# The block exchanges of a one-core decoder layer: issued by GpSimd's queue instead of SyncE's

## The chip, the cores and the metric

The kernel runs on one core of a Trainium2 chip. The metric is the device time of one execution in microseconds, median of several. The engines are named as the profile names them: PE is TensorE, with PEld its weight loads; DVE is VectorE, ACT is ScalarE, POOL is GpSimd, and SP is SyncE, which computes nothing and issues DMAs. A "q" behind a name (SPq, POOLq) means the engine's instruction queue.

## What is computed

One layer of a decoder over 256 tokens of width 2048, in float32: a half SwiGLU, a mixer with attention and spatial gating side by side, another half SwiGLU, and a last norm.

```python
def swiglu(x, w_gate, w_up, w_down):
    return (jax.nn.silu(x @ w_gate) * (x @ w_up)) @ w_down

x = x + 0.5 * swiglu(rmsnorm(x, ffn1_norm), ffn1_w_gate, ffn1_w_up, ffn1_w_down)   # D_FF = 5632
h = rmsnorm(x, mix_norm)
proj = h @ w_in                          # q, k, v, u, v_sg, gate_att, gate_sg
# attention: 3 groups of 4 heads, dilations 1, 4, 16, merged by their denominators
y_att = o_att @ w_att_out
# spatial gating in chunks of 128 positions: u * (W_s LN(v) + b)
y_sg = (u * spatial) @ w_sg_out
x = x + (sigmoid(g_att) * y_att + sigmoid(g_sg) * y_sg) @ w_out
x = x + 0.5 * swiglu(rmsnorm(x, ffn2_norm), ffn2_w_gate, ffn2_w_up, ffn2_w_down)
out = rmsnorm(x, final_norm)
```

## The kernel before

**Products.** Each weight matrix is read once, in units of 512 rows by 512 columns (1 MB, tile `raw`, three buffers, `load_unit`, line 121). A unit is worked off in two half-units of 256 rows. There are 776 half-units, and the program is one loop over them (line 838). To keep float32's precision on the faster float32r path, each half-unit is split: ScalarE rounds the weights to `wh` (line 139), VectorE subtracts to get the rest `wl` (line 140). The activations have been split in the same way (`xhi`, `xlo` and so on). A half-unit is 12 matmuls of 512 columns on TensorE (line 149), per 128 rows and token tile in the order wh·hi, wl·hi, wh·lo. So the first matmul needs `wh` and the second needs `wl`. `wh` and `wl` have four buffers: ScalarE may split three half-units ahead of the one that TensorE works on, and waits for TensorE to release a buffer.

**Exchanges.** A product leaves its result with tokens on the partitions, and the next product needs it with features on the partitions. That turn is done without TensorE, in `turn` (line 168). VectorE transposes 32x32 blocks into a tile `bt...` (`put`, line 191 or 197); one DMA writes the tile to a DRAM tile `bm...` (line 175, 512 KB, 128 partitions of 4 KB); four DMAs read it back with the blocks in turned order (line 181, 128 KB each, into 32 partitions, rows of 1 KB). Then ScalarE and VectorE split what came back (line 163 and 164, or a copy of that kind), which is called the evacuation here. The tiles' names tell the user: `h` is a block of hidden units (22 exchanges, back into `sg`), `x` the residual before a norm (8, into `xt`; there the evacuation begins with ScalarE's line 264), `u`, `q`, `k`, `p` and `m` belong to the mixer (3, 3, 3, 4 and 4), `w` is the spatial weight (2, of 384 KB). That makes 49 exchanges, so 49 writes and 196 reads.

**Order.** All of this order is written out by hand. After the products of half-unit i the loop runs what was registered with `at(i, ...)`: the transposes and the write of an exchange at i, its four reads at i + 3, its evacuation at i + 8, or at i + 6 for x and p. Then `advance` adds the loads and the splits of later half-units. Every engine takes its instructions in that order; a DMA that must wait for data (the reads for the write, the write for the transposes) holds the queue that issues it. SP's queue holds the weight loads, the exchanges and a few constants. POOL's has 18 busy instructions: constants, the powers of the norms (lines 226, 393, 732), the attention mask's rows (lines 341 to 348) and a triangular select of the spatial weights (line 366).

Of the kernel before, what the change touches and what calls it, by code (L numbers as in the profile page):

```python
# [41 lines left out]
def layer(ctx: ExitStack, tc: tile.TileContext, a, out):  # L42
    nc = tc.nc
    PE, ACT, DVE, POOL, SP = nc.tensor, nc.scalar, nc.vector, nc.gpsimd, nc.sync
# [9 lines left out]
    def tp_bank(name):  # L54
        return ps.tile([P, NC], F32, tag="tp", bufs=4, name=name)
# [60 lines left out]
    def at(i, fn):  # L116
        callbacks.setdefault(i, []).append(fn)
# [50 lines left out]
    def turn(i, name, q, put, dst, ev, lag=8):  # L168
        got = {}

        def blocks():
            d = sb.tile([P, 4, q, 32], F32, tag="gate", bufs=2, name=f"bt{name}")
            put(d)
            m = got["m"] = dram.tile([P, 4, q * 32], F32, tag="turn", name=f"bm{name}")
            SP.dma_start(m, d.rearrange("p j m b -> p j (m b)"))

        def back():
            got["e"] = e = dst()
            m = got["m"].rearrange("(i a) j r -> j a i r", a=32)
            for j in range(4):  # L180
                SP.dma_start(e[32 * j:32 * j + 32].rearrange("p (i r) -> p i r", i=4), m[j])

        at(i, blocks)
        at(i + 3, back)
        at(i + lag, lambda: ev(got["e"].rearrange("p (i m b) -> p m i b", i=4, b=32)))
# [589 lines left out]
    b = tp_bank("gc0")  # L775
# [130 lines left out]
```

## Time and profile before

| | us |
|---|---|
| time, median of three runs | 2047.57 (2047.5 to 2048.29) |
| the profiled execution, its own time | 2047.7 |
| its span, first to last instruction | 2046.0 |
| TensorE busy | 2035.8 |
| VectorE busy | 1182.3 |
| ScalarE busy | 974.5 |
| GpSimd busy | 12.5 |

A profile row of an engine gives the start and the length of an instruction in us, the engine, the line of the code, the operation, and the tiles as written<-read; "x4" are four instructions in one row, and a bracket behind it is the idle time before it and who ended it. A DMA's row stands on the queue that issues it and lasts as long as the issue, not as the transfer.

### The profile page before, as it was taken

How to read it: one execution, taken by the hardware profiler on the slowest of the kernel's cores; microseconds unless marked ns; L12 is line 12 of the kernel's file. 1: busy time of each engine (PE TensorE's matmuls, PEld its weight loads, DVE VectorE, ACT ScalarE, POOL GpSimd, SP SyncE). 2: the span in 40 equal slices, each digit the busy share in tenths (PEclk: the TensorE clock that was granted, in tenths of full speed). 3: DMA queues.
4: the chain of work that ended last, by engine and by line, in shares of the span. 5: the costliest groups of instructions: out<-in, count | busy, mean ns of one | idle time of the engine just before them, and what ended most of it. 6: DMA issues, size and time to landing. Idle time of an engine off the chain costs nothing.

```text
span 2046.0 us, 23823 instructions
## 1 busy us (share of the span) xinstructions
PE 2035.8 (100%) x9494; PEld 1781.4 (87%) x9494; DVE 1182.3 (58%) x1193; ACT 974.5 (48%) x1071; POOL 12.5 (1%) x18
## 2 busy tenths in 40 slices
PE   9999999999999999999999999999999999999998
PEld 7888888888888888888888888888888888888887
DVE  5555555455555657665665555565555555555554
ACT  6444444444445555455554444564444444444443
POOL 0000000000000000000000000000000000000000
PEclk9999999999999999999999999999999999999999
DMA  7776876566766855787766666776676656667664
GB/s 271 234 236 226 270 245 216 201 223 225 243 231 217 269 201 202 241 276 261 261 222 220 224 225 206 246 256 231 221 242 224 225 206 205 224 222 240 231 214 144
DMA packets 246775, 469.35 MB, mean 229 GB/s; under 512 B 11084, under 2 KB 38536, under 8 KB 246536
## 3 DMA queue, kind: packets, MB, share of 16 engines
q1 hardware_dynamic: 246344, 467.30, 68.8%
q8 instruction: 74, 1.21, 0.2%
q10 hardware_dynamic: 320, 0.53, 0.1%
q14 instruction: 37, 0.30, 0.0%
HBM read 439.22 MB, written 28.57 MB: 229 GB/s over the span
## 4 chain that ended last, share of the span: by engine, by line
PE 99%; issue 0%; ACT 0%; DVE 0%; POOLq 0%; POOL 0%
PE mm L149 98%; PE sp L458 0%; PE warm L772 0%; PE pv L624 0%; PE sc L587 0%; PE xt L235 0%; PE sc L585 0%; PE pv L620 0%; ACT x L740 0%; ACT xhi L239 0%; PE pv L621 0%; DVE x L725 0%; POOLq L901 0%; POOL rf L732 0%; ACT wh L139 0%
## 5 line engine op out<-in xcount | busy, mean ns | idle before, releaser
L140 DVE TENSOR_TENSOR wl<-raw,wh 128x1024 fp32r<-128x1024 f32 (+1 forms) x780 | 947.6, 1218 | 822.7 <-ACT wh L139 817.6
L139 ACT ACTIVATE wh<-raw 128x1024 fp32r<-128x1024 f32 (+1 forms) x780 | 817.9, 1052 | 1007.6 <-PE mm L149 976.7
L149 PE MATMUL mm<-wh,xhi 128*128 128x512 f32 x2144 | 814.0, 380 | 0.5 <-ACT wh L139 0.4
L149 PE MATMUL mm<-wh,xlo 128*128 128x512 f32 x2144 | 812.5, 379 | 0.0
L149 PE MATMUL mm<-wl,xhi 128*128 128x512 f32 x2144 | 811.8, 379 | 0.0
L149 PEld LDWEIGHTS mm<-wh,xhi 128*128 128x128 f32 x2144 | 405.2, 189 | 58.6 <-ACT wh L139 0.9
L149 PEld LDWEIGHTS mm<-wl,xhi 128*128 128x128 f32 x2144 | 405.4, 189 | 57.3
L149 PEld LDWEIGHTS mm<-wh,xlo 128*128 128x128 f32 x2144 | 405.2, 189 | 57.4
L149 PE MATMUL mm<-wl,hhi 128*128 128x512 f32 x704 | 266.8, 379 | 0.0
L149 PE MATMUL mm<-wh,hhi 128*128 128x512 f32 x704 | 266.8, 379 | 0.0
L149 PE MATMUL mm<-wh,hlo 128*128 128x512 f32 x704 | 266.8, 379 | 0.0
L149 PEld LDWEIGHTS mm<-wl,hhi 128*128 128x128 f32 x704 | 133.1, 189 | 18.9
L149 PEld LDWEIGHTS mm<-wh,hlo 128*128 128x128 f32 x704 | 133.1, 189 | 18.9
L149 PEld LDWEIGHTS mm<-wh,hhi 128*128 128x128 f32 x704 | 133.1, 189 | 18.9
L149 PE MATMUL mm<-wh,uT 128*128 128x512 f32 x192 | 58.0, 379 | 0.0
L149 PE MATMUL mm<-wh,mhi 128*128 128x512 f32 x128 | 48.5, 379 | 0.0
L149 PE MATMUL mm<-wl,mhi 128*128 128x512 f32 x128 | 48.5, 379 | 0.0
L149 PE MATMUL mm<-wh,mlo 128*128 128x512 f32 x128 | 48.5, 379 | 0.0
L149 PEld LDWEIGHTS mm<-wh,uT 128*128 128x128 f32 x192 | 36.3, 189 | 5.1
L149 PE MATMUL mm<-wl,uT 128*128 128x512 f32 x96 | 36.4, 379 | 0.0
L304 DVE SCALAR_TENSOR_TENSOR sg<-mm,rstd,sg 128x512 f32<-128x512 f32 x44 | 30.9, 743 | 0.0
L219 ACT ACTIVATE junk<-x 128x512 bf16<-128x512 f32 x30 | 18.9, 629 | 25.0 <-DVE x L247 18.6
(152 smaller groups left out, 600.6 us busy)
## 6 DMA issues: line engine op xcount, KB each, us to landing
raw<-in_w_in_dram SPq DMA_DIRECT2D x92, 1024.0 KB, 5.0
raw<-in_ffn_w_up_dram SPq DMA_DIRECT2D x88, 1024.0 KB, 5.1
raw<-in_ffn_w_down_dram SPq DMA_DIRECT2D x88, 1024.0 KB, 5.1
raw<-in_ffn_w_gate_dram SPq DMA_DIRECT2D x84, 1024.0 KB, 5.0
raw<-in_w_out_dram SPq DMA_DIRECT2D x16, 1024.0 KB, 5.1
raw<-in_w_sg_out_dram SPq DMA_DIRECT2D x12, 1024.0 KB, 5.7
bmh<-bth SPq DMA_DIRECT2D x22, 512.0 KB, 2.7
sg<-bmh SPq DMA_DIRECT2D x88, 128.0 KB, 4.9
```

Of the source, the lines that this page charges most:

```text
L139: ACT.activation(wh[:, k], r[:, k], AF.Copy)
L140: DVE.tensor_tensor(wl[:, k], r[:, k], wh[:, k].bitcast(F32), op=OP.subtract)
L149: PE.matmul(g["ps"][t], act[:, k, t * P:(t + 1) * P], in_turn(w[:, jj]), start=k == 0 and kind == "hh", stop=k == g["nk"] - 1 and kind == ...
L219: ACT.activation(junk, x[:, t, c * NC:(c + 1) * NC], AF.Square, accum_out=ss[n][:, t, c:c + 1])
L304: DVE.scalar_tensor_tensor(two(sg[:, t]), banks[t], rstd[:, t:t + 1], two(sg[:, t]), op0=OP.mult, op1=OP.mult)
```

## The change

In `turn`, the write and the four reads of every exchange are started from GpSimd's queue. Nothing else is altered: the callbacks, their places, the tiles, the shapes of the transfers and the other engines' orders are the same.

```diff
         def blocks():
             d = sb.tile([P, 4, q, 32], F32, tag="gate", bufs=2, name=f"bt{name}")
             put(d)
             m = got["m"] = dram.tile([P, 4, q * 32], F32, tag="turn", name=f"bm{name}")
-            SP.dma_start(m, d.rearrange("p j m b -> p j (m b)"))
+            POOL.dma_start(m, d.rearrange("p j m b -> p j (m b)"))

         def back():
             got["e"] = e = dst()
             m = got["m"].rearrange("(i a) j r -> j a i r", a=32)
             for j in range(4):
-                SP.dma_start(e[32 * j:32 * j + 32].rearrange("p (i r) -> p i r", i=4), m[j])
+                POOL.dma_start(e[32 * j:32 * j + 32].rearrange("p (i r) -> p i r", i=4), m[j])
```

The orders of TensorE, VectorE and ScalarE are unchanged. On SP's queue, around the exchanges of u and of the first q (`uroom<-bmu` and `q<-bmq`; raw are weight loads of `w_in`), the difference is:

```order
-L175 DMA bmu_6172<-btu_6169 128x1024
 L130 DMA raw_6174<-in_w_in_dram 128x4x512
-L181 DMA uroom<-bmu_6127 32x4x256 x4
-L175 DMA bmu_6220<-btu_6217 128x1024
 L130 DMA raw_6224<-in_w_in_dram 128x4x512
-L181 DMA uroom<-bmu_6172 32x4x256 x4
-L175 DMA bmq_6275<-btq_6272 128x1024
 L130 DMA raw_6277<-in_w_in_dram 128x4x512
-L181 DMA uroom<-bmu_6220 32x4x256 x4
 L130 DMA raw_6317<-in_w_in_dram 128x4x512
-L181 DMA q_6192<-bmq_6275 32x4x256 x4
```

The loads of the weights stand alone on SP there now. On GpSimd's queue at the same place, behind the power of the layer norm (`lnrs`):

```order
 L393 TENSOR_TENSOR lnrs<-ve,half 128x2
+L175 DMA bmu_6127<-btu_6124 128x1024
+L175 DMA bmu_6172<-btu_6169 128x1024
+L181 DMA uroom<-bmu_6127 32x4x256 x4
+L175 DMA bmu_6220<-btu_6217 128x1024
+L181 DMA uroom<-bmu_6172 32x4x256 x4
+L175 DMA bmq_6275<-btq_6272 128x1024
+L181 DMA uroom<-bmu_6220 32x4x256 x4
+L181 DMA q_6192<-bmq_6275 32x4x256 x4
```

The four exchanges follow each other there, each one's reads behind the next one's write. On GpSimd's queue at the first half of the program, where the mask's rows are set and copied (lines 341 to 348), an h exchange now stands ahead of the memset:

```order
+L175 DMA bmh_1730<-bth_1727 128x1024
+L181 DMA sg_1546<-bmh_1730 32x4x256 x4
 L341 MEMSET mask_rows 128x1536
 L347 COPY mask<-mask_rows 128x256
```

The memset waits for the issue of that exchange's reads, and the copies stand ahead of the next exchange.

## Rows read from the trace of the kernel before

**Rows 1.** Part 1 of the page: busy us, share of the span, instructions.

```profile
PE 2035.8 (100%) x9494; PEld 1781.4 (87%) x9494; DVE 1182.3 (58%) x1193; ACT 974.5 (48%) x1071; POOL 12.5 (1%) x18
```

**Rows 2.** Waits of PE: us in total, times, longest us.

```profile
PE mm L149 <- ACT wh L139: 0.4, 1, 0.4
```

**Rows 3.** Lines 175 and 181 by operation: issue ns min/median/max, first and last start.

```profile
L175 SPq DMA_DIRECT2D bmh<-bth x22: 339/344/345, 58.2 to 1940.2; - x22
L181 SPq DMA_DIRECT2D sg<-bmh x88: 303/427/712, 61.5 to 1944.3; - x88
```

**Rows 4.** Part 6 of the page: KB of one, median us from issue to landing.

```profile
bmh<-bth SPq DMA_DIRECT2D x22, 512.0 KB, 2.7
sg<-bmh SPq DMA_DIRECT2D x88, 128.0 KB, 4.9
```

**Rows 5.** Timeline, SP's queue and ACT, the first h exchange: start, length.

```profile
58.19 0.34 SPq L175 DMA_DIRECT2D bmh<-bth  x1
76.31 1.04 ACT L163 ACTIVATE hhi<-sg 128x1024 fp32r<-128x1024 f32 x1
```

**Rows 6.** Timeline of SP's queue, ACT, DVE and PE, third x exchange.

```profile
679.42 0.34 SPq L175 DMA_DIRECT2D bmx<-btx  x1
689.99 1.71 ACT L264 ACTIVATE xt<-xt,gcols 128x256 f32<-128x256 f32 x4 [1.29 <-DMA xt<-bmx]
693.96 3.49 DVE L140 TENSOR_TENSOR wl<-raw,wh 128x1024 fp32r<-128x1024 f32 x3
697.36 0.38 PE L149 MATMUL mm<-wl,xhi 128*128 128x512 f32 x1
```

**Rows 7.** The same for the second and the last x exchange.

```profile
662.15 0.34 SPq L175 DMA_DIRECT2D bmx<-btx  x1
674.14 1.69 ACT L264 ACTIVATE xt<-xt,gcols 128x256 f32<-128x256 f32 x4
679.32 4.80 DVE L140 TENSOR_TENSOR wl<-raw,wh 128x1024 fp32r<-128x1024 f32 x4
681.82 0.38 PE L149 MATMUL mm<-wl,hhi 128*128 128x512 f32 x1
...
1363.31 0.34 SPq L175 DMA_DIRECT2D bmx<-btx  x1
1373.03 1.69 ACT L264 ACTIVATE xt<-xt,gcols 128x256 f32<-128x256 f32 x4
1376.98 2.58 DVE L140 TENSOR_TENSOR wl<-raw,wh 128x1024 fp32r<-128x1024 f32 x2
1382.44 0.38 PE L149 MATMUL mm<-wl,xhi 128*128 128x512 f32 x1
```

**Rows 8.** The u and q exchanges: timeline; windows (PE, PEld, DVE, ACT, POOL, clock, DMA, GB/s); waits.

```profile
843.98 0.34 SPq L175 DMA_DIRECT2D bmu<-btu  x1
873.14 1.36 ACT L163 ACTIVATE qk<-q 128x512 fp32r<-128x512 f32 x2 [0.43 <-DMA q<-bmq]
878.34 3.52 DVE L140 TENSOR_TENSOR wl<-raw,wh 128x1024 fp32r<-128x1024 f32 x3
880.32 0.38 PE L149 MATMUL mm<-wl,xhi 128*128 128x512 f32 x1
...
835.00:875.00 40.00, 40.00 (x192) 35.17 (x191) 28.47 (x46) 20.24 (x23) 0.00 (x0) 1.00 0.90 281
...
ACT wh L139 <- DMA raw<-in_w_in_dram: 8.5, 5, 3.2
```

**Rows 9.** Timeline of POOL, and of DVE beside one of its operations.

```profile
44.35 0.71 POOL L226 TENSOR_TENSOR rstd<-ms,half 128x2 f32<-128x2 f32 x1 [42.98 <-DVE ms L224]
344.38 1.86 POOL L366 TENSOR_SCALAR_AFFINE_SELECT wspT<-wspT 128x1536 f32<-128x1536 f32 x1 [97.29 <-ACT wspT L364]
763.40 1.22 DVE L140 TENSOR_TENSOR wl<-raw,wh 128x1024 fp32r<-128x1024 f32 x1
763.57 1.59 POOL L393 TENSOR_TENSOR lnrs<-ve,half 128x2 f32<-128x2 f32 x1 [60.74 <-DVE ve L391]
```

## The prediction

> **What bounds the kernel now.** I read the first part of the profile's page first: TensorE is busy 2035.8 us of a span of 2046.0 us, and VectorE and ScalarE a little over half of it [rows 1]. The waits of TensorE come next. In the whole program its products wait once for a split weight, 0.4 us [rows 2]. Everything else that is missing from 100% lies in the first 25 us and in the tail. So a faster exchange has nothing to give back: nothing on the way to the end waits for one. The change can only cost, and the question is whether the exchange, issued by GpSimd, still hides.
>
> What hides it is read from the timeline, exchange by exchange. An exchange has a fixed place in the instruction order of four engines: the write at callback i, the four reads at i + 3, the evacuation at i + 8 (i + 6 for the residual's x and attention's p). ScalarE and VectorE take their work in order, so a late landing does not only delay that evacuation: the next weight splits stand behind it. Two margins therefore stand one after the other. The **window** is the time from the write's issue until ScalarE reaches the evacuation. The **cover** is the time by which the next split (wl, which TensorE needs for the second product of a half-unit) is done before TensorE needs it. TensorE stops for lateness beyond window plus cover.
>
> **What the change moves.** 49 writes and 196 reads leave SP's queue and enter GpSimd's, which had 18 instructions and 12.5 us of work. One write on SP takes 0.34 us to issue, one read 0.43 us [rows 3]; from issue to landing a write takes 2.7 us and a read 4.9 us in the median [rows 4]. I keep what comes after the issue: 2.7 - 0.34 = 2.36 us for the write, 4.9 - 0.43 = 4.47 us for the last read. The bytes and the 16 engines that carry them are the same.
>
> The unknown is g, the time that GpSimd takes to issue one DMA; no row of this trace shows one. From below it is bounded by SP's 0.34 us, from above by the longest GpSimd instruction of the trace, the affine select of 1536 columns, 1.86 us. The nearest rows are GpSimd's tiny operations, which measure mostly fixed cost: the 128x2 powers took 0.71, 0.70, 0.69 and 1.59 us, the long one beside a VectorE subtraction that began before it [rows 9]; the first and the long one stand there, the other two read like the first. Their mean is 0.92 us, and I take **g = 0.92**.
>
> With the reads waiting for the write's landing, an exchange lasts g + 2.36 + 4g + 4.47 = 5g + 6.83 us, so **11.4 us** at 0.92; 8.5 us at 0.34, and 16.1 us at 1.86.
>
> *Exchanges of hidden units* (22 h; 4 m and 2 w are like them). The write of the first goes out at 58.19 and ScalarE reaches the evacuation at 76.31: a window of 18.1 us [rows 5]. 11.4 us leaves 6.7 us over, 16.1 us still 2.0. Cost 0 at both ends.
>
> *Exchanges of x* (8, lag 6). The tightest is the third of the first norm: write 679.42, evacuation 689.99, so 10.57 us, and ScalarE already waited 1.29 us of that for the landing. The split behind it ends at 693.96 + 1.22 = 695.18 and TensorE uses it at 697.36: a cover of 2.18 us [rows 6]. Limit: 12.75 us. The one before has 674.14 - 662.15 = 11.99 us and the smallest cover, 681.82 - (679.32 + 1.22) = 1.28 us: limit 13.3 us. The last of the second norm has the shortest window, 1373.03 - 1363.31 = 9.72 us, with 1382.44 - (1376.98 + 1.22) = 4.24 us of cover: limit 14.0 us [rows 7]. 11.4 us passes all three: ScalarE waits 0.8 us more in one and 1.7 us in another, TensorE 0. At g = 0.34 nobody waits; at 1.86 the three cost 3.4, 2.9 and 2.2 us. The other five, read in the same way, have limits between the second of these and 15 us, and the later q, the k and the four p exchanges have longer windows than any x.
>
> *The stretch where four exchanges follow each other* (u0 to u2 and q0). Here GpSimd's order matters most: from u1's write to q0's last read 19 DMAs are issued in a row. u1's write goes out at 843.98 in SP's queue and ScalarE takes q0 at 873.14; the next split ends at 878.34 + 1.22 = 879.56, TensorE uses it at 880.32 [rows 8]. That is 29.16 us and 0.76 us of cover. On GpSimd 19g + 4.47 is 22.0 us at 0.92, so 7 us to spare; at 1.86 it is 39.8 us, and TensorE stops for 10 us.
>
> The small cover there comes from weights, not from the exchange: ScalarE waited 8.5 us in this stretch for raw loads, with the DMA engines 90% busy [rows 8]. In SP's queue the raw loads stand behind the reads, each group of which waits for its own write to land. Once the reads are gone, a raw load goes out as soon as its buffer is free. That gives back up to those 8.5 us of ScalarE waits, and nothing to the end, since TensorE waited for none of them.
>
> *What is queued behind a waiting GpSimd.* A read that waits for its write holds GpSimd for 2.4 us. Behind it stand the power of each norm, whose result the next gate or projection needs eight half-units later; the memset of the mask's rows, now behind an h exchange's reads and four half-units ahead of SP's mask loads, which wait for it; the mask copies; and the select of w_s. None has a user within an exchange's length. The last power, in the tail on the path to the end, comes long after the last exchange. Cost 0; were the memset's cover gone, SP would hold its raw loads for that time. VectorE beside the long power took 1.22 us, its usual time [rows 9], so GpSimd does not slow it.
>
> Two pages of the Trainium skill bear on g and on the latency. DMA: Bandwidth & Descriptors (Specifications) gives about 1 us to the first byte for a DMA from GpSimd and about 0.6 us from SP; no run here shows it yet, and by it an exchange would gain 0.8 us, an estimate of 12.2 us at g = 0.92, still under each limit. SBUF — State Buffer (SBUF: two separate sides) speaks against the change: it warns that GpSimd can't write descriptors while VectorE holds the shared port in a two-port copy, and has 620 ns become 3100 ns. The trace agrees in so far as the power beside the subtraction lasted until that ended; that subtraction, though, is one of the page's two-input operations, which by it hold up only a GpSimd operation that reads SBUF.
>
> **The sum.** 0 on TensorE's path at g = 0.92, nothing gained. The profiled execution of before took 2047.7 us, 0.1 us from the median of 2047.57; I predict **2048.0 us**, with some tenths for an odd wait at the 12.75 us limit.
>
> **Rivals.**
> 1. *GpSimd's issue is held up by VectorE, and its queue becomes the bound.* One mechanism: an issue waits until VectorE's operation ends, as the power that took 1.59 us did. In its favour: that row, and VectorE busy 28.47 of 40 us in the u/q stretch [rows 8]. Against: three of four powers were not held, and an issue reads no tile. It bites from g = 1.18 (5g + 6.83 = 12.75) at the third x, and from (29.16 + 0.76 - 4.47) / 19 = 1.34 in the u/q stretch. At g = 1.6 an exchange lasts 14.8 us: 2.1, 1.6 and 0.9 us at the three x of above, about 2.5 us at the other five, and 34.9 - 29.9 = 5 us in the u/q stretch, 12 us: **2060 us**. At 1.86 it is some 27 us, 2075 us. This is the rival on the other side. The second page's rule is its extreme; by its figure as g an x exchange would last 22 us, which an estimate puts above 2100 us, and since few of VectorE's operations here are such copies I give it no share of its own.
> 2. *The exchange takes DMA time from the raw loads.* On SP's queue the bytes went one after the other; now two queues feed engines that are 90% busy in the u/q stretch. At that stretch's 281 GB/s, 512 KB take 1.9 us, so a raw load beside an exchange's half may land 1.9 us later, against a cover of 0.76 us there: 1.1 us for each of three or four loads, **2052 us**. Against it: the same bytes stood in front of the same loads before, and SP now issues those earlier. It decides only where a raw load is the last thing to land.
> 3. *The freed SP queue speeds the kernel.* The raw loads come earlier, but TensorE's only wait on a split is 0.4 us [rows 2]: at best **2047 us**, within the bound of no change.
> 4. *The DMAs do not go where the change says.* The order shows them on GpSimd, and SP's queue without them; I give it nothing.
>
> **How the numbers follow.** A measurement of this kernel can tell about 0.2% from no change, 4.1 us. My forecast (all hidden, 2047 to 2051) has 0.62, rival 1 0.27, rival 2 0.07 and rival 3 0.04, of which half within the bound. Rival 1 passes 4.1 us from g of about 1.45; nearly all of it is slower, and of rival 2 nearly half (0.03 is given to slower). Of the forecast 0.05 goes to slower for several x exchanges that each lose some tenths. So faster 0.02, same 0.63, slower 0.35. The range reaches from 2046.5, below which only a twentieth lies, to 2065, which is g of about 1.7; above it stands the rest of rival 1, about 0.1.
>
> **What would show it.** On GpSimd 245 DMA rows of about 0.9 us each; an x exchange of 11 to 12 us from issue to landing; ScalarE waiting for landings of x a few times, by 1 to 2 us; TensorE's waits on splits still under 1 us in all; fewer and shorter waits for raw loads between 835 and 880. I am wrong if the GpSimd rows take over 1.2 us, if TensorE waits for splits at 697, 682, 1382 or 880, or if the landings come later than 4.5 us behind an issue though the issues are short.

## The result and the profile after

The changed kernel takes **2051.54 us** in the median of 18 runs (2050.47 to 2055.72), the kernel before 2047.66 us in the runs beside it. The ratio is 1.002, with a 95% interval of 1.0013 to 1.0028: a loss of 3.9 us, just inside the 0.2% (4.1 us) that the prediction called no change, though the interval itself excludes 1. The forecast of 2048.0 us was 3.5 us too low; the range of 2046.5 to 2065 us holds the result. The profiled execution took 2051.38 us at a span of 2049.7 us, against 2047.7 and 2046.0 us.

Part 1 of the page of the changed kernel (busy us, share of the span, instructions):

```profile
PE 2037.1 (99%) x9494; PEld 1781.4 (87%) x9494; DVE 1182.2 (58%) x1193; ACT 974.2 (48%) x1071; POOL 148.7 (7%) x263
```

GpSimd has 245 instructions more than in [rows 1], the 245 DMAs; the rival in which the change does not do what it says is out. Their price (lines 175 and 181, ns min/median/max), for the write of h and the reads of h and x:

```profile
L175 POOL DMA_DIRECT2D bmh<-bth x22: 558/558/731, 58.6 to 1944.4; - x22
...
L181 POOL DMA_DIRECT2D sg<-bmh x88: 550/550/572, 62.4 to 1950.1; - x88
L181 POOL DMA_DIRECT2D xt<-bmx x32: 550/550/568, 650.2 to 1373.4; - x32
```

So g is 0.55 to 0.56 us in the median of each group; the longest of all 245 took 0.79 us. Part 6 (KB of one, median us from issue to landing) has the answers to [rows 4]:

```profile
bmh<-bth POOLq DMA_DIRECT2D x22, 512.0 KB, 3.3
sg<-bmh POOLq DMA_DIRECT2D x88, 128.0 KB, 3.6
```

Writes land 0.6 us later than from SP; the reads of h land 1.3 us earlier, so a queue of its own is not slow in itself. Where the time went is read from the waits of TensorE (us in total, times, longest us), against the one wait of [rows 2]:

```profile
PE mm L149 <- DVE wl L140: 1.9, 2, 1.0
...
PE mm L149 <- ACT wh L139: 0.9, 2, 0.6
```

and from the stretch where they lie. First TensorE from 640 to 735 us in the windows view of the kernel before (length, PE busy with the number of products, clock, DMA share, GB/s):

```profile
640.00:735.00 95.00, 95.00 (x442) 1.00 0.74 245
```

and the same of the changed kernel:

```profile
640.00:735.00 95.00, 92.45 (x425) 1.00 0.72 237
```

17 products fewer fit into the same 95 us. One takes 95 / 442 = 0.215 us, so 3.7 us are lost here, and that is the whole difference of the two profiled executions (2051.38 - 2047.7). Up to 2000 us the counts of all other stretches agree to within one product. The waits named above come to less, 1.9 + 0.9 - 0.4 = 2.4 us, because a wait is counted from the end of the product before: that takes 0.38 us and more, while the next can start after 0.215 us. Now the timeline of the changed kernel at the third and the fourth x exchange of the first norm (start, length, engine, line; idle time and what ended it):

```profile
680.65 0.56 POOL L175 DMA_DIRECT2D bmx<-btx  x1 [11.66 <-DVE btx L191]
681.38 5.89 SPq L130 DMA_DIRECT2D raw<-in_w_in_dram  x3
685.35 2.21 POOL L181 DMA_DIRECT2D xt<-bmx  x4 [4.14 <-DMA bmx<-btx]
694.26 1.71 ACT L264 ACTIVATE xt<-xt,gcols 128x256 f32<-128x256 f32 x4 [4.72 <-DMA xt<-bmx]
698.05 0.48 PE L149 MATMUL mm<-wh,xhi 128*128 128x512 f32 x1 [0.58 <-ACT wh L139]
698.23 3.49 DVE L140 TENSOR_TENSOR wl<-raw,wh 128x1024 fp32r<-128x1024 f32 x3
699.50 0.48 PE L149 MATMUL mm<-wl,xhi 128*128 128x512 f32 x1 [0.97 <-DVE wl L140]
706.22 1.30 DVE L191 STREAM_TRANSPOSE btx<-x 128x512 f32<-128x512 f32 x2
707.92 0.61 POOL L175 DMA_DIRECT2D bmx<-btx  x1 [0.80 <-DVE btx L191]
712.20 2.21 POOL L181 DMA_DIRECT2D xt<-bmx  x4 [3.66 <-DMA bmx<-btx]
721.70 1.70 ACT L264 ACTIVATE xt<-xt,gcols 128x256 f32<-128x256 f32 x4 [5.51 <-DMA xt<-bmx]
726.94 0.48 PE L149 MATMUL mm<-wl,xhi 128*128 128x512 f32 x1 [0.97 <-DVE wl L140]
```

The third exchange lasts 694.26 - 680.65 = 13.6 us, where the forecast had 11.4; ScalarE waits 4.72 us for it (1.29 us in [rows 6]), its splits are late, and TensorE reaches the product with wl at 699.50 us. In [rows 6] that product stood at 697.36 us; this execution ran 681.99 - 681.82 = 0.17 us behind before the stretch, so 1.97 us are lost. The fourth lasts 721.70 - 707.92 = 13.8 us and loses another 1.5 us. The rows of the kernel before, SP's queue at the third exchange and then the fourth (timeline of SP, ACT, DVE and PE):

```profile
680.53 0.37 SPq L130 DMA_DIRECT2D raw<-in_w_in_dram  x1
682.30 2.11 SPq L181 DMA_DIRECT2D xt<-bmx  x4
684.51 2.62 SPq L130 DMA_DIRECT2D raw<-in_w_in_dram  x2
...
701.95 1.30 DVE L191 STREAM_TRANSPOSE btx<-x 128x512 f32<-128x512 f32 x2
703.28 0.34 SPq L175 DMA_DIRECT2D bmx<-btx  x1
713.85 1.69 ACT L264 ACTIVATE xt<-xt,gcols 128x256 f32<-128x256 f32 x4
717.80 2.58 DVE L140 TENSOR_TENSOR wl<-raw,wh 128x1024 fp32r<-128x1024 f32 x2
723.26 0.38 PE L149 MATMUL mm<-wl,xhi 128*128 128x512 f32 x1
```

The u and q stretch, which the prediction feared most, is quiet. ScalarE's waits for raw loads from 835 to 880 us, 8.5 us in [rows 8], are

```profile
ACT wh L139 <- DMA raw<-in_w_in_dram: 0.8, 1, 0.8
```

in the changed kernel, and TensorE waits for nothing there.

### The profile page after: what moved, and what is told of

Read it like the earlier page. It is cut to its first block, busy times and chain, and to the rows that moved or that the text cites. A ratio compares the mean times of both kernels' runs of the same rounds, so it can differ in the third digit from the quotient of the medians.

```text
span 2049.7 us, 23909 instructions
## 1 busy us (share of the span) xinstructions
PE 2037.1 (99%) x9494; PEld 1781.4 (87%) x9494; DVE 1182.2 (58%) x1193; ACT 974.2 (48%) x1071; POOL 148.7 (7%) x263
## 4 chain that ended last, share of the span: by engine, by line
PE 64%; issue 2%; DMA 1%; DVE 0%; POOL 0%; ACT 0%; POOLq 0%; ACTq 0%
PE mm L149 63%; DMA xt<-bmx 1%; DMA bmx<-btx 1%; POOL xt L181 0%; DVE wl L140 0%; PE sp L458 0%; PE pv L624 0%; PE sc L587 0%; ACT xt L264 0%; PE sc L585 0%; ACT xhi L163 0%; DVE xlo L164 0%; PE pv L620 0%; ACT x L740 0%; ACT wh L139 0%
## 5 line engine op out<-in xcount | busy, mean ns | idle before, releaser
L175 POOL DMA_DIRECT2D bmh<-bth x22 | 12.5, 568 | 908.1 <-DVE bth L191 908.1
L181 POOL DMA_DIRECT2D sg<-bmh x88 | 48.6, 553 | 77.3 <-DMA bmh<-bth 77.1
```

Source lines behind the costliest of these rows:

```text
L175: POOL.dma_start(m, d.rearrange("p j m b -> p j (m b)"))
L181: POOL.dma_start(e[32 * j:32 * j + 32].rearrange("p (i r) -> p i r", i=4), m[j])
```

## The experiments

The theory after this reading: an x exchange from GpSimd lasts 2 to 4 us longer, in part because SP's queue, freed of the reads, sends later raw loads out beside them; only those exchanges that pass their limit cost anything. The rivals: a small loss in every exchange; GpSimd's latency alone; room for the descriptors that GpSimd writes. The medians of the kernel before beside these runs were 2047.64 us (first four), 2047.74 us (next four) and 2047.73 us (last four).

### Which exchanges cost

Two exchanges go back to SP (x1_2 and x1_3 are the third and fourth of the first norm; for the next kernel the second, x1_1, joins them):

```diff
-            POOL.dma_start(m, d.rearrange("p j m b -> p j (m b)"))
+            (SP if name in ("x1_2", "x1_3") else POOL).dma_start(m, d.rearrange("p j m b -> p j (m b)"))
...
-                POOL.dma_start(e[32 * j:32 * j + 32]...
+                (SP if name in ("x1_2", "x1_3") else POOL).dma_start(e[32 * j:32 * j + 32]...
```

> Only the third and fourth x exchange of the first norm (x1_2, x1_3) go back to SyncE's queue; the other 47 exchanges stay with GpSimd. Theory 1 (the loss is at these two alone, where the landing comes later than TensorE's margin allows): TensorE's waits between 698 and 727 us go, the time falls by 3.8 us to that of the kernel before, 2047.7 us. Rival A (GpSimd's issue costs a little in every exchange, 49 of them at 0.08 us each): 2 of 49 give back 0.2 us, 2051.4 us. Rival B (the freed SyncE queue brings raw loads earlier and they disturb ScalarE or VectorE all over): nearly the same as with the change, 2051 us.

Measured: 2049.22 us, ratio 1.0007 (0.9998 to 1.0017). Two of 49 exchanges give back 2.3 us of 3.9 (the slowest of the ten runs, 2050.49 us, is as long as the fastest with the change), which a loss spread over all does not allow, but not the 3.8 us that the theory wanted. The windows view shows the stretch still 4 products short:

```profile
640.00:735.00 95.00, 94.40 (x438) 1.00 0.74 244
```

They are lost at 682 us: this time x1_1, still on GpSimd, lasted 675.84 - 662.22 = 13.6 us, past its limit of 13.3. So that one went back too.

> The second, third and fourth x exchange of the first norm (x1_1, x1_2, x1_3) go back to SyncE's queue, the other 46 exchanges stay with GpSimd. With only the last two back, TensorE still waited once, at 682 us, for x1_1, whose last read landed 7.2 us behind its issue. Theory 1 (whoever lands beyond its limit costs, nobody else): that wait goes too, no wait on a split beyond the head of the program, 2047.7 us. Rival A (something is lost in every exchange that GpSimd issues): 2049 us, as with two of them back.

Measured: 2047.78 us, ratio 0.9999 (0.999 to 1.0009), as the theory had it; 46 exchanges from GpSimd cost nothing that can be measured. The profiled execution itself took 2048.75 us, though, and lost 9 products at another place, the last x exchange of the second norm (the changed kernel has 419 products in this window, as the kernel before):

```profile
640.00:735.00 95.00, 95.00 (x442) 1.00 0.76 247
...
1310.00:1400.00 90.00, 88.69 (x410) 1.00 0.75 245
```

"No wait on a split beyond the head" was therefore wrong for this execution: which exchange loses time changes from one execution to the next. This one took 1378.15 - 1365.11 = 13.0 us, under the prediction's 14.0, but its write went out at 1365.11 us, 2.6 us late against [rows 7] (the execution was 0.8 us ahead there), which leaves a limit of 11.4 us. The opposite edit, "POOL" and "SP" exchanged in the first diff:

> The other way round: only x1_2 and x1_3 are issued by GpSimd, the other 47 exchanges by SyncE. Theory 1: the whole loss is there, 2051.5 us, with TensorE waiting about 1 to 1.5 us four times between 698 and 727. Rival A: 2047.8 us. If the loss is in part due to raw loads that the emptied SyncE queue brings earlier from farther back, something between, 2049 us.

Measured: 2049.76 us, ratio 1.001 (1.0001 to 1.0019). These two alone cost about 2.1 us, not 3.9: with x1_1 on time, x1_2's write goes out earlier. In the profiled execution, 2050.76 us long, 8 products are missing here and 8 or 9 in the u and q stretch, which no edit touched (windows; the kernel before has 140 products in the second one):

```profile
640.00:735.00 95.00, 94.03 (x434) 1.00 0.74 244
860.00:890.00 30.00, 28.96 (x132) 1.00 0.94 274
```

The same kernel and the kernel before were therefore profiled once more, unchanged.

> The kernel with only x1_2 and x1_3 on GpSimd, unchanged, profiled a second time. If the 1.5 us that TensorE lost at 876 to 884 us is the stretch's variation between executions: another amount there, perhaps none, and 1 to 3 us at 698 to 727 as before. If it follows from the two exchanges: again 1 to 2 us at 876 to 884.

> The kernel before, unchanged, profiled a second time, for the stretch at 876 to 884 us where its cover is 0.76 us: with only x1_2 and x1_3 on GpSimd TensorE lost 1.5 us there, though nothing of that stretch was changed. If this stretch varies from one execution to the next, TensorE waits there for some tenths here too, or the cover differs from 0.76 us by several tenths; if not, cover 0.7 to 0.8 us and no wait.

Measured: 2049.61 us with nothing lost at 860 to 890 us and 10 products at the x exchanges; and 2048.06 us for the kernel before, where TensorE waited some 0.1 us at 880 us, its cover of 0.76 us used up. So this is the stretch's own variation while the reads stand in SP's queue. That it comes from raw loads is argued, not shown: ScalarE waited for them 8.5 us in [rows 8], 11.2 us in the second execution of the kernel before, 11.2 and 5.7 us in the two of this kernel, and the same 11.2 us cost 8 products in one and none in the other.

### The write or the reads

Only one of the two lines is changed back.

> GpSimd issues only the write of each exchange; the four reads stay in SyncE's queue, so raw loads stand behind them as before. Theory 1: the exchange gets longer by GpSimd's late start (about 0.5 us), its longer issue (0.2 us) and its longer time to landing (0.3 to 0.9 us), in sum 1.0 to 1.6 us; the third x exchange then ends within about 12.5 us of its limit of 12.75 us, and the time is 2047.7 to 2048.2 us. Rival C (nearly all of the loss is GpSimd's own latency in the write): 2050.5 us or more.

Measured: 2047.95 us, ratio 1.0001 (0.9992 to 1.0011), and all 442 products. The write alone is within the theory's 2047.7 to 2048.2 us and can't be told from the kernel before; rival C, the write's latency as the whole loss, falls.

> SyncE issues the write, GpSimd the four reads. The reads start 0.6 us later behind the write's landing, take 0.5 us longer to issue, and share the DMA engines with raw loads that SyncE now issues beside them. Theory 1: the reads land 1.5 to 3 us later than in the kernel before at x1_2 and x1_3, TensorE loses 1 to 2 us there, 2048.7 to 2050 us. Rival C (the write's latency is the loss): 2047.7 us. Rival D (sharing with raw loads is all of it): 2051 us.

Measured: 2052.21 us, ratio 1.0022 (1.0012 to 1.0031), as much as the whole change costs (the intervals overlap). The theory's 2048.7 to 2050 us was too low; rival D's 2051 us is nearer. The profiled execution was the fastest of the ten, 2050.30 us, so it holds only 2.6 us of the 4.6 us that the median lost. The reads of x1_2 and x1_3 in this kernel (line 181: issue ns, then us from issue to landing):

```profile
L181 POOL DMA_DIRECT2D xt<-bmx x8: 550/550/598, 682.9 to 711.9; - x8
...
DMA to landing us min/median/max: 5.8/8.1/8.8
```

The same two exchanges in the kernel before:

```profile
L181 SPq DMA_DIRECT2D xt<-bmx x8: 327/432/781, 682.3 to 707.4; - x8
...
DMA to landing us min/median/max: 4.4/5.9/6.2
```

The reads' landing is 2.2 us later in the median at 0.1 us more issue time. With the write alone moved it is 6.0 us in the median, as before.

### GpSimd's latency or the raw loads beside

Two kernels separate these. In the first, everything is issued by GpSimd, and SP is held until the reads of x1_2 and x1_3 have landed:

```diff
                 POOL.dma_start(e[32 * j:32 * j + 32]...
+            if name in ("x1_2", "x1_3"):
+                SP.dma_start(dram.tile([P, 8], F32, tag="hold", ...), e[:, 0:8])
```

> All exchanges by GpSimd, but behind the reads of x1_2 and x1_3 SyncE issues a small DMA (8 columns of xt to DRAM) that must wait for the reads' landing: SyncE issues no raw load beside these reads. Theory 1 with sharing (raw loads beside the reads take their DMA time): the last read lands 3 to 4 us behind its issue instead of 6 to 7 us, the exchange takes 10 to 11 us, and TensorE's waits at 698 to 727 go, 2047.7 us; if the held raw loads come late in turn, TensorE waits for them instead, up to 2050 us. Rival E (GpSimd's reads are late by themselves, whoever shares the engines): the reads still land 6 us or more behind their issue, 2051 us or more.

The rows of line 181 for these two exchanges:

```profile
L181 POOL DMA_DIRECT2D xt<-bmx x8: 550/550/565, 685.9 to 712.4; - x8
...
DMA to landing us min/median/max: 3.7/4.1/4.4
```

and of the changed kernel:

```profile
L181 POOL DMA_DIRECT2D xt<-bmx x8: 550/551/568, 685.3 to 713.9; - x8
...
DMA to landing us min/median/max: 6.3/7.1/7.7
```

From the same queue, with the same issue time, the reads land in 4.1 us instead of 7.1 us. Rival E falls. The two exchanges last 11.6 and 11.2 us instead of 13.6 and 13.8. The time, 2049.37 us (ratio 1.0006, 0.9997 to 1.0016), recovers 2.2 us of the 3.9: the stretch is still 5 products short. ScalarE scales xt in place, so it now waits for the holding DMA to have read it, and for a raw load that was held:

```profile
ACT wh L139 <- DMA raw<-in_w_in_dram: 4.5, 1, 4.5
...
ACT xt L266 <- DMA holdx<-xt: 1.6, 1, 1.6
```

(waits of ACT from 686 to 702 us). So this kernel shows where the reads' lateness comes from; what its absence is worth to the whole time it does not show cleanly, and the other 1.7 us stay open here.

In the second kernel ScalarE's queue issues all 245 DMAs ("ACT" for "POOL" in both lines): a queue of its own again, but no GpSimd.

> All 245 DMAs of the exchanges are issued by ScalarE's queue: also a queue apart from SyncE's raw loads, but without GpSimd. The reads then wait for the write's landing within ScalarE's own order and hold its work. Theory 1 with sharing: the landing times beside raw loads are as with GpSimd (5 to 7 us behind the issue at x1_2 and x1_3), but the issue and the start are shorter; how much ScalarE's waiting for the writes' landings costs is not known from any row, 2 to 3 us of ScalarE's time at each of 49 exchanges, of which its idle time hides most: 2048 to 2060 us. Rival E: the reads land as fast as from SyncE with nothing beside them, 3 to 4 us.

```profile
L181 ACTq DMA_DIRECT2D xt<-bmx x8: 389/455/761, 681.9 to 709.4; - x8
...
DMA to landing us min/median/max: 2.8/7.4/8.6
```

The landing is as late as with GpSimd, 7.4 us in the median, at SP's issue time. So the late landing belongs to reads in a queue beside SP's at this place, not to GpSimd. The time, 2053.95 us (ratio 1.003, 1.0019 to 1.0041), holds other losses too: TensorE waits 1.5 and 0.9 us in the attention, behind ScalarE's work, and several times for some tenths to 1 us at 855 to 885 us.

### The margin

The evacuation of each x exchange one callback later, all exchanges from GpSimd:

```diff
-             lambda: flat(sb.tile([P, NT, NC], F32, tag="gate", bufs=2, name=f"xt{n}_{c}")), evac, 6)
+             lambda: flat(sb.tile([P, NT, NC], F32, tag="gate", bufs=2, name=f"xt{n}_{c}")), evac, 7)
```

> All exchanges by GpSimd as in the changed kernel, but the evacuation of each x exchange stands one callback later (i + 7 instead of i + 6), so that its window grows by one place, some 1.5 to 2 us. Theory 1 (the landing passes the margin by 1 to 1.5 us at two exchanges): TensorE's waits between 698 and 727 shrink to under 1 us in all, 2047.7 to 2048.5 us. Rival A (a cost that is spread over all exchanges): 2051.5 us. A third outcome: the evacuation meets the next place where VectorE or ScalarE is late, and part of the loss moves there, 2049 to 2050 us.

Measured: 2047.49 us, ratio 0.9998 (0.9988 to 1.0007); the whole loss is gone, though x1_2 and x1_3 still land 13.0 and 14.4 us behind their write's issue. The windows view:

```profile
640.00:735.00 95.00, 95.00 (x442) 1.00 0.76 245
```

The same edit in the kernel before is the control.

> The kernel before, every exchange in SyncE's queue, with the evacuation of the x exchanges one callback later (i + 7). Theory 1: nobody waited for x in the kernel before, so the later place gives nothing, 2047.6 us, and the recovery that the later place brought with GpSimd is all from the landing. Rival G (the later place is better by itself, by 1 us or more, and hid a cost of GpSimd's that remains): 2046.5 us or less.

Measured: 2047.64 us, ratio 1.0 (0.999 to 1.0009). The later place is worth nothing by itself; with GpSimd it made up for the late landing. Neither version with the later place can be told from the kernel before, so nothing here beats both kernels.

### Room for descriptors

```diff
-    pad = big.tile([P, 96], F32, name="pad")
+    pad = big.tile([P, 32], F32, name="pad")
...
-... dynamic_dma_scratch_size=1024)
+... dynamic_dma_scratch_size=2048)
```

> All exchanges by GpSimd, with twice the room for the descriptors that GpSimd writes (2048 instead of 1024 bytes in each partition; an unused padding tile is cut by 64 columns to make room). Theory 1: room for descriptors holds nothing here, 2051.5 us, and writes and reads are issued in 0.55 us as before. Rival F (GpSimd's queue waits for room, and that is what makes the reads start and land late): the start behind the write's landing falls from 0.65 us to about 0.1 us and the time to about 2049 us.

Measured: 2050.63 us, ratio 1.0013 (1.0004 to 1.0023). The interval overlaps the changed kernel's, the reads land in 6.9 us in the median and are issued in 0.55 us as before, and the start of the reads behind the write's landing is 0.1 us shorter, not 0.5: rival F has no support. Whether the 0.9 us between the two medians is real stays open.

### One sum over all profiled executions

Products missing in the three stretches, times 0.215 us, against each profiled execution's own time less 2047.7 us:

| kernel | 640 to 735 | 860 to 890 | 1310 to 1400 | lost, us | time over 2047.7, us |
|---|---|---|---|---|---|
| changed kernel | 17 | 0 | 0 | 3.7 | 3.7 |
| two on SP | 4 | 0 | 0 | 0.9 | 0.9 |
| two on GpSimd | 8 | 8 | 0 | 3.4 | 3.1 |
| write on GpSimd | 0 | 0 | 0 | 0 | 0.1 |
| reads on GpSimd | 11 | 0 | 2 | 2.8 | 2.6 |
| evacuation later | 0 | 0 | 0 | 0 | -0.4 |
| SP held | 5 | 0 | 0 | 1.1 | 1.2 |
| twice the room | 9 | 0 | 4 | 2.8 | 2.6 |
| three on SP | 0 | 0 | 9 | 1.9 | 1.1 |
| before, evacuation later | 0 | 12 | 0 | 2.6 | 2.3 |
| two on GpSimd, again | 10 | 0 | 0 | 2.2 | 1.9 |
| kernel before, again | 0 | 0 | 0 | 0 | 0.4 |

The kernel with ScalarE's queue is left out, since it loses time elsewhere too. The three stretches were chosen where losses had been seen; their missing products explain each of the others to within 0.9 us, whatever was changed. The table also shows that one profile is not the median: "before, evacuation later" was profiled in a run of 2050.03 us, its slowest, at a median of 2047.64 us.

## Why the prediction was right or wrong

**What bounds the kernel: right.** TensorE remains the bound, there was nothing to give back, and the method (window plus cover for each exchange) named both the place and the signs: TensorE waiting for a split at 697 us was listed as what would prove the forecast wrong, and it did wait there (699.50 us here).

**g: wrong in size, on the safe side.** 0.92 us was taken from GpSimd's tiny arithmetic; it measured 0.55 to 0.56 us. The mean left out GpSimd's two smallest powers (line 732, 128x1), 0.55 us each; no run shows whether their nearness is more than chance. Rival 1 (issue held by VectorE) falls with the spread: 88 reads between 550 and 572 ns, with VectorE busy 58% of the span. The power on which it rested ended at 765.16 us, 0.54 us behind the subtraction's end at 764.62, not with it. The trap for which SBUF — State Buffer (SBUF: two separate sides) of the Trainium skill was named does not show in any of these rows.

**The terms behind the issue: this step failed.** They were kept at SP's values, 2.36 and 4.47 us. For the third exchange, term by term (forecast, measured): write issue 0.92, 0.56; write to landing 2.36, 3.3 (3.9 us from issue to landing, less 0.56); landing to first read 0, 0.8; four reads 3.68, 2.21; last read (its issue ends at 687.56 us) to ScalarE 4.47, 694.26 - 687.56 = 6.7. The sums are 11.4 and 13.6 us. The short issue saves 1.8 us and the other three terms cost 1.0, 0.8 and 2.2 us. Part of the last was to be seen in advance: 4.47 us came from the median of the reads of h. The same formula with SP's own issue times gives 0.34 + 2.36 + 4 x 0.43 + 4.47 = 8.9 us, while [rows 6] put SP's third x exchange at 10.57 us, ScalarE waiting for it. From the end of SP's last read there to ScalarE were 689.99 - 684.41 = 5.6 us, so 1.1 of the 2.2 us were in the trace of before; the term came from the wrong exchange. The rest came with the change.

**Rival 2: the right contention, the wrong victim.** It had the exchange take DMA time from the raw loads. What cost time was the other side: the raw loads, sent earlier by the freed SP queue, delay the reads, as the kernel with SP held shows. The timeline above has SP issue three raw loads between 681.38 and 687.27 us, around the reads of 685.35 us; in the kernel before, SP sent one at 680.53 us ahead of the reads, and its order kept the next, at 684.51 us, behind them. The raw loads sent in this stretch land later too (median 7.0 against 6.0 us from issue to landing), but ScalarE waits only 0.7 us more for one (2.87 against 2.19 us). The prediction said that raw loads would come earlier and did not follow what they would then meet. The Trainium skill, DMA: Bandwidth & Descriptors (Queues, rings and completion order), has each DMA engine take turns between the rings for which it has work. The 7.1, 7.4 and 4.1 us of GpSimd's queue, ScalarE's queue and GpSimd's queue with SP held agree with that; by this rule a moved read no longer has the earlier place in the line.

**The limits were not independent.** Each was worked out with the write at the place of the kernel before. But ScalarE's wait of one exchange delays VectorE, and the next write stands behind VectorE's work. At the fourth exchange the sum of window and cover before was 713.85 - 703.28 + 723.26 - (717.80 + 1.22) = 14.8 us, and 13.8 us would stay within it. From write to product, however, there were 723.26 - 703.28 = 19.98 us before. In the changed kernel the product was due at 725.40 us (723.26 + 0.17 + 1.97) and the write went out at 707.92: 17.48 us. 0.4 us of the 2.5 us lost is GpSimd's slower start behind the transposes, 2.1 us is VectorE, whose transposes stand 4.27 us later (701.95, 706.22) while TensorE is 2.14 us later. So the limit was 12.3 us, and 13.8 us exceeds it by 1.5 us. At the third exchange the same two effects take 0.4 and 0.7 us from the limit of 12.75, which leaves 11.65, and 13.6 us exceeds it by about the 1.97 us lost there.

**The u and q stretch: wrong way round.** It was to be at risk; its waits for raw loads almost vanish (0.8 us), and with them the losses of up to 2.6 us that it has in some executions with the reads on SP. Rival 3 has this much truth. It does not show in the median of the kernel before; of three profiled executions with every exchange on SP, two lose at most 0.2 us there.

**The chances.** The class of no change had 0.63 and came true by 0.2 us, but not by the case that carried it: "all hidden" was false, so that the class and the range held the result is luck. The 0.05 for "several x exchanges that each lose some tenths" was the nearest to what happened, and too small: two exchanges lost 2.0 and 1.5 us, since at each of them several terms were late together.

## What to carry to other kernels

A queue's order is also a priority: reads that stand ahead of later loads in one queue lose that place when they move to another, so ask first what the emptied queue will send out earlier and whom it meets. It need not be a loss at every place: here the reads of h landed earlier from their own queue, those of x1_2 and x1_3 later. Work out a margin with the worst row of the exchange concerned, not with the median of another, and shift the start of each margin by the lateness of the one before it. Here, where a margin was short by 1.5 to 2 us, one place more between issue and use cost nothing that can be measured and restored all of it.

## What the runs showed of the hardware

- GpSimd issues a DMA of 128 KB or 512 KB in 0.55 to 0.56 us in the median (the longest of 245 took 0.79) beside a VectorE that is busy 58% of the time; SP takes 0.34 and 0.43 us.
- GpSimd reacts late to what it waits for: the first read starts 0.8 us behind the write's landing (680.65 + 3.9 to 685.35 us), against 0.1 us on SP, and the write 0.4 us behind the transposes (706.22 + 1.30 to 707.92 us), against 0.03 us on SP. Its write of 512 KB lands 3.3 us after the start of the issue in the median, against 2.7 us. The Trainium skill, DMA: Bandwidth & Descriptors (Specifications), puts 0.4 us between the two paths for the first byte. For a write of this kernel, start and landing together differ by more, 0.4 + 0.6 = 1.0 us, of which 0.2 us is the longer issue.
- The same 128 KB reads (x1_2, x1_3) take 4.1 us to landing in the median with SP held, 7.1 us without, both from GpSimd. The reads of h, of the same size, take 3.6 us from GpSimd and 4.9 us from SP.
